# A decoder layer on one core: the last FFN projection in pairs of column blocks with seven products for eight

## The chip, the cores and the metric

The kernel runs on one core of a Trainium2 chip. The metric is the device time of one execution in microseconds; before the change it is 1440.92 us, the median of three runs (1440.82 to 1441.05).

## What is computed

One decoder layer on 256 tokens of width 2048, in float32: a combined input projection, a retention branch and a sliding-window attention branch, gates, an output projection and a layer norm, and then the channel-mixing sublayer, the only part that the change touches. Its end is

```
h = layer_norm(DEEPNORM_ALPHA * h + merged @ w_out, ln1_g, ln1_b)
ffn = (silu(h @ w_gate) * (h @ w_up)) @ w_down
h = layer_norm(DEEPNORM_ALPHA * h + ffn, ln2_g, ln2_b)
```

with `w_gate` and `w_up` 2048 x 5632 and `w_down` 5632 x 2048. Call p = silu(h @ w_gate) * (h @ w_up); it is 256 x 5632.

## The kernel before

**Products.** Every weight block and every activation is kept as a high and a low part (`wh`, `wl`, and `hh`, `hl` for h, `ph`, `pl` for the transposed p), rounded to the matmul's input type. One product of a 128 x 128 activation tile with a 128 x 512 weight block is three matmuls: high by high, high by low, low by high. All matmuls of this kind have the same size.

**Chunks.** A `Stream` walks through chunks. A plain `Chunk` is one block of 512 output columns: for every four k tiles one 1 MB weight block is loaded (`raw`), cast to `wh` by ScalarE (L217), reduced to `wl` by VectorE (L218), and used by 24 matmuls (four k tiles, two token halves, three matmuls each; L233 to L235). Its two accumulators are added to the residual by `resid` (L881).

A `PairChunk` takes two column blocks and works in k pairs: one 1 MB block holds two k tiles of both column blocks. A block of kind "s" is done as before, 8 products. A block of kind "S" is treated as a 2 x 2 matrix product (k tile by column block, token half by k tile) with seven products, in two steps: R, three products with weights as they are (9 matmuls), and T, four products with sums of weights (12 matmuls). The sums are formed by VectorE (L290, L291, L292 into `tsum`), cast by ScalarE into `th` and reduced by VectorE into `tl` (L304, L305), and the activations for them are sums too (`sh`, `sl`, made by `hsums`). Seven accumulators and an eighth for the plain blocks fill all eight PSUM banks; after the last T step `mids` (L734 to L738) combines the products P1, P5, P6 and P7, and after the last step the four C accumulators are added.

**The FFN.** There are 11 blocks of 512 columns of p, in three parts of 4, 4 and 3. For f = 0 gate and up are two plain chunks; for f = 1 to 10 they are one `PairChunk` (gate and up as the two column blocks) with eight blocks, three S and five s, in the order S s S s S s s s. After the blocks of a part come four plain chunks of `w_down` (c = 0 to 3), whose k range is that part. `done_gu` forms p for its block (L962 to L969), and `u_bg`, a background job, transposes it (L540) and splits it into `ph` and `pl` (L401, L402). The blocks of one chunk f are transposed while the next one runs; those of the last f of a part (3, 7, 10) while the first chunk of `w_down` runs.

**What sets the order.** Loads and casts are issued ahead of the matmuls as far as buffers allow: three `raw` blocks, three `wh`/`wl` pairs, one `th`/`tl` pair, one `tsum`. Background jobs advance a fixed number of steps after every step of a chunk. From this program order the framework's scheduler fixes the order of each engine's queue when the kernel is built; on the chip each queue runs in that order. A transposition, a plain matmul and an accumulator all draw on the same pool of eight banks.

Of the kernel before, what the change touches and what calls it, by code (L numbers as in the profile page):

```python
# [99 lines left out]
def layer_kernel(ctx, tc, a, out):  # L100
# [807 lines left out]
    def done_u(ch, t, c):  # L908
        sg = sgf[c]
        nc.vector.tensor_mul(out=sg[:, t], in0=sg[:, t], in1=ch.acc[t])  # L910
        if t == 0:
            pTs[c] = (sc["pp"].tile([P, 4, SEQ], F32R, name="ph"), sc["pp"].tile([P, 4, SEQ], F32R, name="pl"))
        Job(u_bg(sg, t, *pTs[c]))

    def u_bg(sg, t, ph, pl):
        yield
        yield
        ps = transpose4([sg[:, t, i * P:(i + 1) * P] for i in range(4)])
        yield
# [12 lines left out]

    def lhs_s(kp, i):
        return sc["sh"][:, i, kp], sc["sl"][:, i, kp]

    def hsums(hh, hl, sh, sl_, n):
        for kp in range(n):
            h2 = sc["tp"].tile([P, 2, 2, P], F32, name="s1")
            sm = sc["tp"].tile([P, 4, P], F32, name="vx")
            ks = slice(2 * kp, 2 * kp + 2)  # L940
            nc.vector.tensor_add(out=h2.rearrange("p k t c -> p k (t c)"), in0=hh[:, ks].bitcast(F32), in1=hl[:, ks].bitcast(F32))
            nc.vector.tensor_add(out=sm[:, 0], in0=h2[:, 0, 1], in1=h2[:, 1, 1])
            nc.vector.tensor_sub(out=sm[:, 1], in0=sm[:, 0], in1=h2[:, 0, 0])
            nc.vector.tensor_sub(out=sm[:, 2], in0=h2[:, 0, 1], in1=h2[:, 0, 0])
            nc.vector.tensor_sub(out=sm[:, 3], in0=h2[:, 1, 0], in1=sm[:, 1])
            split_evict(sh[:, :, kp], sl_[:, :, kp], sm)
            yield

    def mid_gu(ch):
# [1 line left out]
        flush()  # L951

    def flush():
        for arg in ev.pop("u", []):
            Job(u_bg(*arg))

    def done_gu(ch, f):
        acc = ch.acc
        s1, vx, w, x5 = ev["t"]
        sg = sc["fp"].tile([P, 2, C], F32, name="sg2", bufs=1)  # L960
        pTs[f] = (sc["pp"].tile([P, 4, SEQ], F32R, name="ph"), sc["pp"].tile([P, 4, SEQ], F32R, name="pl"))
        nc.vector.tensor_add(out=sg[:, 0], in0=s1, in1=acc["C11"])  # L962
        nc.scalar.activation(out=sg[:, 0], in_=sg[:, 0], func=AF.Silu)
        nc.vector.tensor_add(out=w, in0=w, in1=acc["C12"])
        nc.vector.tensor_add(out=sg[:, 1], in0=vx, in1=acc["C21"])
        nc.scalar.activation(out=sg[:, 1], in_=sg[:, 1], func=AF.Silu)
        nc.vector.tensor_mul(out=sg[:, 0], in0=sg[:, 0], in1=w)
        nc.vector.tensor_add(out=x5, in0=x5, in1=acc["C22"])
        nc.vector.tensor_mul(out=sg[:, 1], in0=sg[:, 1], in1=x5)  # L969
        ev["u"] = [(sg, t, *pTs[f]) for t in range(2)]  # L970
        if f + 1 in (4, 8, 11):
            flush()

    parts = ((0, 4), (4, 8), (8, 11))
# [24 lines left out]

    i = 0  # L1000
# [152 lines left out]
```

## Time and profile before

| | |
|---|---|
| time, median of three runs | 1440.92 us (1440.82 to 1441.05) |
| the profiled execution | 1440.99 us, of which the span of the trace is 1439.2 us |
| TensorE busy (PE) | 1432.2 us, 100% of the span |
| weight loads (PEld) | 1174.7 us, 82% |
| VectorE busy (DVE) | 1047.2 us, 73% |
| ScalarE busy (ACT) | 673.9 us, 47% |
| loaded from HBM | 271.60 MB, 190 GB/s over the span |

Busy time of PE is modelled from pipelined instructions: a matmul's row lasts 0.39 us, but the next one starts about 0.23 us after it. Whether PE loses time is therefore read from the starts of its matmuls and not from its share. On VectorE, too, rows overlap a little: an instruction takes the engine for the distance from its start to the start of the next one, if nothing is waited for.

### The profile page before, as it was taken

The page shows a single profiled execution, that of the slowest core. Times are in us where ns is not written, and L with a number is a line of the kernel's source. Part 1 is how long each engine was busy: PE and PEld are TensorE (multiplying, and loading weights), DVE is VectorE, ACT ScalarE, POOL GpSimd, SP SyncE. Part 2 cuts the span into 40 slices and gives each one's busy share as a digit, 9 for nine tenths or more (in the row PEclk, how much of TensorE's full clock was granted, in tenths as well). Part 3 has the DMA queues.
Part 4 walks back from the last instruction along what each step waited for, and adds up shares of the span by engine and source line. Part 5 has one row for each costly group of instructions (what it writes and reads, how often), then busy time and mean ns, then how long its engine had stood idle before and what let it go on. Part 6 is the DMA issues. An engine that isn't in the chain of part 4 may idle for free.

```text
span 1439.2 us, 16027 instructions
## 1 busy us (share of the span) xinstructions
PE 1432.2 (100%) x6536; PEld 1174.7 (82%) x6536; DVE 1047.2 (73%) x1127; ACT 673.9 (47%) x637; POOL 0.9 (0%) x6
## 2 busy tenths in 40 slices
PE   9999999999999999999999999999999999999998
PEld 7878888878878878788888888888888888888886
DVE  6764555487879879766688996567898755799756
ACT  5465444344545445444355454344555434454432
POOL 0000000000000000000000000000000000000000
PEclk9999999999999999999999999999999999999999
DMA  8643433455555655577445645555655555555562
GB/s 325 226 152 117 147 117 118 146 178 209 198 204 179 216 189 200 182 282 262 161 144 205 228 181 193 188 196 191 227 180 208 194 178 204 205 198 207 195 223 83
DMA packets 40233, 274.73 MB, mean 191 GB/s; under 512 B 4704, under 2 KB 4832, under 8 KB 8160
## 3 DMA queue, kind: packets, MB, share of 16 engines
q1 hardware_dynamic: 39440, 272.79, 53.3%
q8 instruction: 51, 0.84, 0.2%
q10 hardware_dynamic: 720, 0.92, 0.2%
q14 instruction: 22, 0.18, 0.0%
HBM read 271.60 MB, written 2.10 MB: 190 GB/s over the span
## 4 chain that ended last, share of the span: by engine, by line
PE 98%; DVE 1%; DMA 0%; ACT 0%; SPq 0%; issue 0%
PE bank L324 16%; PE bank L326 16%; PE bank L325 16%; PE acc L235 9%; PE acc L233 9%; PE acc L234 9%; PE bank L234 6%; PE bank L235 6%; PE bank L233 6%; PE tr L540 2%; PE mx L589 1%; PE mx L618 1%; PE bank L540 1%; DMA xraw<-in_xw 0%; PE bank L685 0%; PE mx L656 0%
## 5 line engine op out<-in xcount | busy, mean ns | idle before, releaser
L218 DVE TENSOR_TENSOR wl<-raw,wh 128x2048 fp32r<-128x2048 f32 x108 | 247.1, 2290 | 171.8 <-ACT wh L217 171.5
L304 ACT CAST wh<-raw 128x2048 fp32r<-128x2048 f32 (+1 forms) x136 | 241.2, 1773 | 229.2 <-PE bank L326 161.6
L217 ACT CAST wh<-raw 128x2048 fp32r<-128x2048 f32 x108 | 206.2, 1910 | 301.7 <-PE acc L235 108.5
L305 DVE TENSOR_TENSOR wl<-raw,wh 128x2048 fp32r<-128x2048 f32 (+1 forms) x136 | 287.0, 2115 | 61.7 <-ACT wh L304 61.2
L324 PE MATMUL bank<-wh,hh 128*128 128x512 f32 x460 | 179.6, 391 | 0.0
L326 PE MATMUL bank<-wh,hl 128*128 128x512 f32 x460 | 179.1, 389 | 0.0
L325 PE MATMUL bank<-wl,hh 128*128 128x512 f32 x460 | 179.0, 389 | 0.0
L324 PE MATMUL bank<-wh,xh 128*128 128x512 f32 x364 | 144.5, 397 | 0.0
L326 PE MATMUL bank<-wh,xl 128*128 128x512 f32 x364 | 141.8, 389 | 0.0
L325 PE MATMUL bank<-wl,xh 128*128 128x512 f32 x364 | 141.7, 389 | 0.0
L233 PE MATMUL acc<-wh,xh 128*128 128x512 f32 x352 | 141.0, 402 | 0.0
L235 PE MATMUL acc<-wh,xl 128*128 128x512 f32 x352 | 138.7, 394 | 0.0
L234 PE MATMUL acc<-wl,xh 128*128 128x512 f32 x352 | 137.9, 392 | 0.5 <-DVE wl L218 0.5
L233 PE MATMUL bank<-wh,ph 128*128 128x512 f32 x352 | 137.2, 390 | 0.0
L235 PE MATMUL bank<-wh,pl 128*128 128x512 f32 x352 | 137.0, 389 | 0.0
L234 PE MATMUL bank<-wl,ph 128*128 128x512 f32 x352 | 136.9, 389 | 0.0
L305 DVE TENSOR_TENSOR tl<-tsum,th 128x2048 fp32r<-128x2048 f32 x44 | 100.8, 2290 | 21.4 <-ACT th L304 21.1
L304 ACT CAST th<-tsum 128x2048 fp32r<-128x2048 f32 x44 | 84.2, 1914 | 63.1 <-DVE tsum L292 42.9
L326 PEld LDWEIGHTS bank<-wh,hl 128*128 128x128 f32 x460 | 86.4, 188 | 18.0
L324 PEld LDWEIGHTS bank<-wh,hh 128*128 128x128 f32 x460 | 86.4, 188 | 17.8
L325 PEld LDWEIGHTS bank<-wl,hh 128*128 128x128 f32 x460 | 86.4, 188 | 17.7
L324 PEld LDWEIGHTS bank<-wh,xh 128*128 128x128 f32 x364 | 68.3, 188 | 15.8 <-issue 1.4
(250 smaller groups left out, 2100.2 us busy)
## 6 DMA issues: line engine op xcount, KB each, us to landing
raw<-in_w_gu SPq DMA_DIRECT2D x88, 1024.0 KB, 4.9
raw<-in_w_ip SPq DMA_DIRECT2D x56, 1024.0 KB, 4.9
raw<-in_w_down SPq DMA_DIRECT2D x44, 1024.0 KB, 4.9
raw<-in_w_in SPq DMA_DIRECT2D x40, 1024.0 KB, 4.9
raw<-in_w_out SPq DMA_DIRECT2D x16, 1024.0 KB, 5.2
xraw<-in_xw SPq DMA_DIRECT2D x7, 768.0 KB, 6.7
hres<-in_x SPq DMA_DIRECT2D x1, 2048.0 KB, 7.5
out_h<-hres SPq DMA_DIRECT2D x5, 256.0 KB, 2.4
```

What stands on the lines that cost most here:

```text
L217: nc.scalar.copy(out=h[:, 0:m], in_=r)
L218: nc.vector.tensor_sub(out=l[:, 0:m], in0=r, in1=h[:, 0:m].bitcast(F32))
L233: nc.tensor.matmul(self.acc[t], lhsT=xh, rhs=wh[:, j], start=st, stop=False)
L234: nc.tensor.matmul(self.acc[t], lhsT=xh, rhs=wl[:, j], start=False, stop=False)
L235: nc.tensor.matmul(self.acc[t], lhsT=xl, rhs=wh[:, j], start=False, stop=sp)
L304: nc.scalar.copy(out=h_, in_=r)
L305: nc.vector.tensor_sub(out=l_, in0=r, in1=h_.bitcast(F32))
L324: nc.tensor.matmul(self.acc[p], lhsT=xh, rhs=wh[:, j], start=st, stop=False)
L325: nc.tensor.matmul(self.acc[p], lhsT=xh, rhs=wl[:, j], start=False, stop=False)
L326: nc.tensor.matmul(self.acc[p], lhsT=xl, rhs=wh[:, j], start=False, stop=sp)
L540: m = nc.tensor.transpose(ps[:, i], s, ident)
L589: nc.tensor.matmul(sps[u][:, i], lhsT=qT[u * HD:(u + 1) * HD, h // 2], rhs=kT[u * HD:(u + 1) * HD, g, 0:W], start=True, stop=True)
```

## The change

The four `w_down` chunks of a part become pair chunks. In parts 0 and 1, columns 0 and 1, and 2 and 3, each make one `PairChunk` of eight blocks, three of them S; in part 2, columns 0 and 1 make one of six blocks, two of them S, and columns 2 and 3 stay plain chunks. The weights are laid out for it on the host (`w_dp`, `w_dl`); the blocks stay 1 MB each and 44 in number. The sums of the transposed activations (`psh`, `psl`, two k pairs from the first block of a part, one from the second in parts 0 and 1) are made by a new background job, `psums`, queued behind the transposition of that block. The residual is now added in two steps: `mid_d` adds the four middle results to it, `done_dp` the four C accumulators (and in part 2 takes the statistics of columns 0 and 1).

```diff
-    def pair_seq(n):
+    def pair_seq(n, nkp=KT // 2):
...
-        return sq + [("s", kp) for kp in range(2 * n, KT // 2)]
+        return sq + [("s", kp) for kp in range(2 * n, nkp)]
...
+    parts = ((0, 4), (4, 8), (8, 11))
+    NS = (3, 3, 2)
...
-        Job(u_bg(sg, t, *pTs[c]))
+        ujobs.append(Job(u_bg(sg, t, *pTs[c])))
+        if t:
+            queue_p(c, ujobs)
...
-        if half == 2 and c == CP and t == 1:
-            nc.vector.tensor_mul(out=sc["zg"], in0=sc["hres"][:, t, c * C:(c + 1) * C], in1=gains["ln2_g"][:, c * C:(c + 1) * C])
...
+    def mid_d(ch, part, cp):
+        mids(ch)
+        for i, v in enumerate(ev["t"][j] for j in (0, 2, 1, 3)):
+            z = sc["hres"][:, i // 2, (2 * cp + i % 2) * C:(2 * cp + i % 2 + 1) * C]
+            if part:
+                nc.vector.tensor_add(out=z, in0=z, in1=v)
+            else:
+                nc.vector.scalar_tensor_tensor(out=z, in0=z, scalar=ALPHA, in1=v, op0=ALU.mult, op1=ALU.add)
+
+    def done_dp(ch, part, cp):
+        for t in range(2):
+            for u in range(2):
+                c = 2 * cp + u
+                z = sc["hres"][:, t, c * C:(c + 1) * C]
+                nc.vector.tensor_add(out=z, in0=z, in1=ch.acc[f"C{t + 1}{u + 1}"])
+        if part == 2:
+            for t in range(2):
+                for c in (2 * cp, 2 * cp + 1):
+                    nc.vector.bn_stats(out=sc["stats"][:, t, c], in_=sc["hres"][:, t, c * C:(c + 1) * C])
...
+    def psums(ph, pl, k0, n):
+        yield
+        yield from hsums(ph, pl, sc["psh"], sc["psl"], n, k0)
...
+    def queue_p(f, js):
+        kp = 2 * (f - f0_of[f])
+        n = min(2, ND[f] - kp)
+        if n > 0:
+            jobs["ps", f] = Job(psums(*pTs[f], kp, n), js)
...
-        for c in range(4):
-            stream.add(Chunk([a["w_down"][c, f0 + b] for b in range(nk // KB)], nk, lhs_p, lambda ch, t, part=part, c=c: done_d(ch, t, part, c),
-                             order=stagger(NSPL) if part == 2 and c == 3 else None))
+        for cp in range(2 if part < 2 else 1):
+            stream.add(PairChunk([a["w_dp"][cp, 2 * f0 + kp] for kp in range(nk // 2)], pair_seq(NS[part], nk // 2), lhs_p, lhs_ps,
+                                 lambda ch, part=part, cp=cp: mid_d(ch, part, cp), lambda ch, part=part, cp=cp: done_dp(ch, part, cp)))
+        if part == 2:
+            for c in (2, 3):
+                stream.add(Chunk([a["w_dl"][c - 2, b] for b in range(nk // KB)], nk, lhs_p, lambda ch, t, part=part, c=c: done_d(ch, t, part, c),
+                                 order=stagger(NSPL) if c == 3 else None))
```

The change moves work in the queues at three kinds of places. The first is VectorE at the end of a part. Before, at the end of chunk f = 3, p (`sg2`) is finished (L962 to L969) among the `wl` of the plain chunks:

```order
L218 TENSOR_TENSOR wl_6420<-raw_6313,wh_6419 128x2048
L962 TENSOR_TENSOR sg2_6449<-s1_6342,bank_6183 128x512
L964 TENSOR_TENSOR w_6344<-w_6344,bank_6187 128x512
L965 TENSOR_TENSOR sg2_6449<-vx_6343,bank_6203 128x512
L967 TENSOR_TENSOR sg2_6449<-sg2_6449,w_6344 128x512
L968 TENSOR_TENSOR x5_6345<-x5_6345,bank_6222 128x512
L218 TENSOR_TENSOR wl_6461<-raw_6328,wh_6460 128x2048
L969 TENSOR_TENSOR sg2_6449<-sg2_6449,x5_6345 128x512
L218 TENSOR_TENSOR wl_6507<-raw_6393,wh_6506 128x2048
L402 TENSOR_TENSOR pl_6451<-bank_6492,ph_6450 128x4x128
```

In the changed kernel the same place (L999 to L1006 there) reads, with the sums of the weights of the pair chunk in between:

```order
L305 TENSOR_TENSOR wl_6460<-raw_6345,wh_6459 128x2048
L999 TENSOR_TENSOR sg2_6489<-s1_6374,bank_6215 128x512
L1001 TENSOR_TENSOR w_6376<-w_6376,bank_6219 128x512
L1002 TENSOR_TENSOR sg2_6489<-vx_6375,bank_6235 128x512
L1004 TENSOR_TENSOR sg2_6489<-sg2_6489,w_6376 128x512
L1005 TENSOR_TENSOR x5_6377<-x5_6377,bank_6254 128x512
L292 TENSOR_TENSOR tsum_6500<-raw_6360,tsum_6500 128x512
L1006 TENSOR_TENSOR sg2_6489<-sg2_6489,x5_6377 128x512
L305 TENSOR_TENSOR wl_6505<-raw_6360,wh_6504 128x1536
L402 TENSOR_TENSOR pl_6491<-bank_6520,ph_6490 128x4x128
```

The last product (L969, now L1006) stands behind a short sum instead of a whole `wl`; on PE the eight transpositions that read it moved from behind the first 24 matmuls of the `w_down` chunk to behind its first 9 and, the second four, 5 more.

The second is VectorE in the middle of the `w_down` work. Before, in a plain chunk, the queue holds only `wl` and the two additions to the residual:

```order
L218 TENSOR_TENSOR wl_6567<-raw_6464,wh_6566 128x2048
L881 SCALAR_TENSOR_TENSOR hres_4761<-hres_4761,bank_6466 128x512
L881 SCALAR_TENSOR_TENSOR hres_4761<-hres_4761,bank_6470 128x512
L218 TENSOR_TENSOR wl_6599<-raw_6510,wh_6598 128x2048
L218 TENSOR_TENSOR wl_6631<-raw_6540,wh_6630 128x2048
```

Now, at the start of the second pair chunk of part 0 (L952 is `done_dp` of the first):

```order
L305 TENSOR_TENSOR wl_6761<-raw_6656,wh_6760 128x2048
L952 TENSOR_TENSOR hres_4761<-hres_4761,bank_6512 128x512
L952 TENSOR_TENSOR hres_4761<-hres_4761,bank_6516 128x512
L952 TENSOR_TENSOR hres_4761<-hres_4761,bank_6546 128x512
L952 TENSOR_TENSOR hres_4761<-hres_4761,bank_6565 128x512
L290 TENSOR_TENSOR tsum_6794<-raw_6671 128x1024
L305 TENSOR_TENSOR wl_6799<-raw_6671,wh_6798 128x1536
L291 TENSOR_TENSOR tsum_6794<-raw_6671,tsum_6794 128x512
L305 TENSOR_TENSOR wl_6837<-raw_6734,wh_6836 128x2048
L292 TENSOR_TENSOR tsum_6794<-raw_6671,tsum_6794 128x512
L305 TENSOR_TENSOR tl_6831<-tsum_6794,th_6830 128x2048
```

The weight sums of the chunk's second S block now stand behind the four additions, and the last of them behind the `wl` of a plain block; `tl` follows directly on it.

The third is PE in the gate and up chunk after the `w_down` work of part 0 (f = 4), at its second T step. Before:

```order
L326 MATMUL bank_6994<-wh_6982,sl_4765 128x512
L324 MATMUL bank_6998<-th_7014,sh_4764 128x512
L325 MATMUL bank_6998<-tl_7015,sh_4764 128x512
L326 MATMUL bank_6998<-th_7014,sl_4765 128x512
L324 MATMUL bank_7002<-th_7014,sh_4764 128x512
L325 MATMUL bank_7002<-tl_7015,sh_4764 128x512
```

Now:

```order
L324 MATMUL bank_7094<-th_7110,sh_4764 128x512
L324 MATMUL bank_7098<-th_7110,sh_4764 128x512
L324 MATMUL bank_7102<-th_7110,sh_4764 128x512
L324 MATMUL bank_7106<-th_7110,hh_4762 128x512
L324 MATMUL bank_7090<-wh_7116,hh_4762 128x512
L325 MATMUL bank_7090<-wl_7117,hh_4762 128x512
L326 MATMUL bank_7090<-wh_7116,hl_4763 128x512
L324 MATMUL bank_7125<-wh_7116,hh_4762 128x512
L325 MATMUL bank_7125<-wl_7117,hh_4762 128x512
L325 MATMUL bank_7094<-tl_7111,sh_4764 128x512
L326 MATMUL bank_7094<-th_7110,sl_4765 128x512
```

The four matmuls of the step that need only `th`, and five of the following plain block, moved ahead of the first that needs `tl`.

## Rows read from the trace of the kernel before

**Rows 1.** The page, parts 1 and 2: busy time, granted TensorE clock by slice.

```profile
PE 1432.2 (100%) x6536; PEld 1174.7 (82%) x6536; DVE 1047.2 (73%) x1127; ACT 673.9 (47%) x637; POOL 0.9 (0%) x6
...
PEclk9999999999999999999999999999999999999999
```

**Rows 2.** The page, part 4: shares of the chain that ended last, by engine.

```profile
PE 98%; DVE 1%; DMA 0%; ACT 0%; SPq 0%; issue 0%
```

**Rows 3.** That chain in time order (start, duration, engine, tile, line).

```profile
1052.18 0.87 PE bank L540 x8
1094.58 0.87 PE bank L540 x8
1136.96 0.87 PE bank L540 x8
1154.20 0.87 PE bank L540 x8
...
1428.93 0.24 PE bank L235
...
1434.56 0.75 DVE hres L834
```

**Rows 4.** Busy time by stretch: `w_down` of part 0, then gate/up of part 1.

```profile
core 0: us, PE busy (x) PEld busy (x) DVE busy (x) ACT busy (x) POOL busy (x), PEclk, DMA share, GB/s
892.00:980.00 88.00, 88.00 (x394) 72.97 (x393) 51.93 (x37) 33.73 (x21) 0.00 (x0) 1.00 0.56 192
...
1000.00:1128.00 128.00, 128.00 (x575) 106.14 (x574) 112.51 (x94) 66.10 (x47) 0.00 (x0) 1.00 0.56 200
```

**Rows 5.** VectorE in order of time, around the end of gate/up chunk f = 5.

```profile
1028.31 2.29 DVE L305 TENSOR_TENSOR tl<-tsum,th 128x2048 fp32r<-128x2048 f32 x1 [0.21 <-ACT th L304]
...
1056.60 1.75 DVE L305 TENSOR_TENSOR wl<-raw,wh 128x1536 fp32r<-128x1536 f32 x1
1058.27 1.22 DVE L290 TENSOR_TENSOR tsum<-raw 128x1024 f32<-128x1024 f32 x1
1059.53 0.69 DVE L291 TENSOR_TENSOR tsum<-raw,tsum 128x512 f32<-128x512 f32 x1
1060.25 0.69 DVE L292 TENSOR_TENSOR tsum<-raw,tsum 128x512 f32<-128x512 f32 x1
1060.86 2.29 DVE L305 TENSOR_TENSOR wl<-raw,wh 128x2048 fp32r<-128x2048 f32 x1
1063.06 0.68 DVE L962 TENSOR_TENSOR sg<-s,bank 128x512 f32<-128x512 f32 x1
1063.66 0.68 DVE L964 TENSOR_TENSOR w<-w,bank 128x512 f32<-128x512 f32 x1
```

**Rows 6.** PE in order of time: the second T step of chunk f = 5.

```profile
1033.65 0.39 PE L324 MATMUL bank<-th,sh 128*128 128x512 f32 x1
1033.87 0.39 PE L325 MATMUL bank<-tl,sh 128*128 128x512 f32 x1
```

**Rows 7.** VectorE making sums of activations (`hsums`) for gate/up.

```profile
749.52 0.29 DVE L942 TENSOR_TENSOR vx<-s 128x128 f32<-128x128 f32 x1
749.73 0.28 DVE L944 TENSOR_TENSOR vx<-s 128x128 f32<-128x128 f32 x1
```

**Rows 8.** ScalarE in order of time, chunk f = 4: two casts of weights.

```profile
1009.95 1.91 ACT L304 CAST th<-tsum 128x2048 fp32r<-128x2048 f32 x1 [5.21 <-DVE tsum L292]
1011.76 1.47 ACT L304 CAST wh<-raw 128x1536 fp32r<-128x1536 f32 x1
```

**Rows 9.** VectorE, then PE, in order of time at the end of part 0.

```profile
896.39 0.69 DVE L969 TENSOR_TENSOR sg<-sg,x 128x512 f32<-128x512 f32 x1
...
897.44 1.03 PE L540 MATMUL bank<-cst,sg 128*128 128x128 f32 x8
```

**Rows 10.** The page, part 6: loads of weight blocks, us from issue to landing.

```profile
raw<-in_w_gu SPq DMA_DIRECT2D x88, 1024.0 KB, 4.9
```

**Rows 11.** VectorE in the first gate/up pair chunk, f = 1: a wait for `th`.

```profile
785.33 2.29 DVE L305 TENSOR_TENSOR tl<-tsum,th 128x2048 fp32r<-128x2048 f32 x1 [2.06 <-ACT th L304]
```

More of the change, by code (lines that the diff above doesn't have):

```diff
@@ L901, in layer_kernel @@
     sgf = {}
+    ujobs = []
+    parts = ((0, 4), (4, 8), (8, 11))
+    NS = (3, 3, 2)
+    f0_of = {f: f0 for f0, f1 in parts for f in range(f0, f1)}
+    ND = {f: n for (f0, f1), n in zip(parts, NS) for f in range(f0, f1)}
     def done_g(ch, t, c):
@@ L927, in done_d, with hsums @@
         resid(ch, t, c, 1.0 if half else ALPHA, half == 2)
-        if half == 2 and c == CP and t == 1:
-            nc.vector.tensor_mul(out=sc["zg"], in0=sc["hres"][:, t, c * C:(c + 1) * C], in1=gains["ln2_g"][:, c * C:(c + 1) * C])
         if half == 2 and c == 3:
             ln2(t)
+    def mid_d(ch, part, cp):
[16 more added lines that the diff above has]
+                    nc.vector.bn_stats(out=sc["stats"][:, t, c], in_=sc["hres"][:, t, c * C:(c + 1) * C])
+            nc.vector.tensor_mul(out=sc["zg"], in0=sc["hres"][:, 1, CP * C:(CP + 1) * C], in1=gains["ln2_g"][:, CP * C:(CP + 1) * C])
     def lhs_s(kp, i):
         return sc["sh"][:, i, kp], sc["sl"][:, i, kp]
-    def hsums(hh, hl, sh, sl_, n):
+    def psums(ph, pl, k0, n):
+        yield
+        yield from hsums(ph, pl, sc["psh"], sc["psl"], n, k0)
+    def hsums(hh, hl, sh, sl_, n, k0=0):
         for kp in range(n):
@@ L945, in hsums @@
             nc.vector.tensor_sub(out=sm[:, 3], in0=h2[:, 1, 0], in1=sm[:, 1])
-            split_evict(sh[:, :, kp], sl_[:, :, kp], sm)
+            split_evict(sh[:, :, k0 + kp], sl_[:, :, k0 + kp], sm)
             yield
@@ L953, in flush @@
     def flush():
-        for arg in ev.pop("u", []):
-            Job(u_bg(*arg))
+        if "u" in ev:
+            f, args = ev.pop("u")
+            queue_p(f, [Job(u_bg(*arg)) for arg in args])
+    def queue_p(f, js):
[3 more added lines that the diff above has]
+            jobs["ps", f] = Job(psums(*pTs[f], kp, n), js)
     def done_gu(ch, f):
@@ L969, in done_gu @@
         nc.vector.tensor_mul(out=sg[:, 1], in0=sg[:, 1], in1=x5)
-        ev["u"] = [(sg, t, *pTs[f]) for t in range(2)]
+        ev["u"] = f, [(sg, t, *pTs[f]) for t in range(2)]
         if f + 1 in (4, 8, 11):
             flush()
-    parts = ((0, 4), (4, 8), (8, 11))
     seq = pair_seq(NQ)
@@ L993, in lhs_p, with lhs_ps @@
             return ph[:, k % 4, t * P:(t + 1) * P], pl[:, k % 4, t * P:(t + 1) * P]
-        for c in range(4):
-            stream.add(Chunk([a["w_down"][c, f0 + b] for b in range(nk // KB)], nk, lhs_p, lambda ch, t, part=part, c=c: done_d(ch, t, part, c),
-                             order=stagger(NSPL) if part == 2 and c == 3 else None))
+        def lhs_ps(kp, i, f0=f0):
+            assert jobs["ps", f0 + kp // 2].over
+            return sc["psh"][:, i, kp], sc["psl"][:, i, kp]
+        for cp in range(2 if part < 2 else 1):
[5 more added lines that the diff above has]
+                                 order=stagger(NSPL) if c == 3 else None))
     i = 0
@@ L1062, in layer_kernel @@
     sc["sp2"] = ppc.enter_context(tc.tile_pool(name="sp2", bufs=1, side=RIGHT))
+    pq = ppc.enter_context(tc.tile_pool(name="pq", bufs=1, side=RIGHT))
+    sc["psh"] = pq.tile([P, 4, max(NS), P], F32R, name="psh")
+    sc["psl"] = pq.tile([P, 4, max(NS), P], F32R, name="psl")
     Job(hsums(sc["hh"], sc["hl"], sc["sh"], sc["sl"], NQ))
@@ L1139 @@
         "w_gu": _pairs(g["w_gate"][0][:, C:], g["w_up"][0][:, C:]),
-        "w_down": _blocks(g["w_down"][0]),
+        "w_dp": _pairs(np.concatenate([g["w_down"][0][:, 2 * i * C:(2 * i + 1) * C] for i in range(2)], axis=1),
+                       np.concatenate([g["w_down"][0][:, (2 * i + 1) * C:(2 * i + 2) * C] for i in range(2)], axis=1)),
+        "w_dl": _blocks(g["w_down"][0][8 * C:, 2 * C:]),
         "gn_g": g["ret_gn_g"], "gn_b": g["ret_gn_b"],
```

## The prediction

> **What bounds the kernel now.** I read busy time first: PE is busy 100% of the span, VectorE 73% [rows 1]. A busy PE proves little, since its rows overlap; so next the chain that ended last, 98% of which is PE [rows 2], and then the starts of matmuls. From the transpositions at 1052.18 to those at 1094.58 lies one gate/up chunk: 183 matmuls (three S blocks of 21, five s blocks of 24) and eight transpositions in 42.40 us. From 1136.96 to 1154.20, across the end of part 1, lie 72 matmuls and eight transpositions in 17.24 us [rows 3]. The difference is 111 matmuls in 25.16 us, 0.2267 us each, and eight transpositions with what surrounds them take 0.92 us. The first T row and its neighbour start 0.22 us apart too, though the second waits for `tl` [rows 6]. PE thus has one pace in plain and pair chunks, with no gap, at a granted clock of nine tenths or more in every slice [rows 1], the 2.4 GHz level. A matmul less is 0.2267 us less, as long as nothing else becomes late.
>
> What could become late is VectorE. In the `w_down` work it is busy 51.93 of 88 us, in the gate/up chunks 112.51 of 128 [rows 4]: 59% and 88%. The change gives the first the load of the second.
>
> **The change, part by part.** *Matmuls removed.* S blocks: 2 chunks x 3 in part 0, the same in part 1, 1 x 2 in part 2, so 14, each with one product of three matmuls less: 42 x 0.2267 = 9.52 us. All of it is on the path. By the Trainium skill's page "TensorE: Matmul & The Clock Gate" (section Back-to-back issue gap) a stream of 512-column matmuls runs at about 131 ns each, or 216 ns for an isolated gap; that would make the sum 5.5 or 9.1 us. The trace's 0.2267 us decides, and is used here.
>
> *Work added on VectorE and ScalarE.* The price of an instruction is the distance to the next start [rows 5]: 2.20 for a 128x2048 `wl` or `tl`, 1.67 for 128x1536, 1.26 or less for L290, 0.72 and 0.61 for L291 and L292, 0.60 for 128x512, and 0.21 for 128x128 [rows 7]. Each S block adds sums 2.6 and `tl` 2.2 and saves 0.5 on its `wl`: 14 x 4.3 = 60 us. Each of five pairs has twelve 128x512 operations where four stood: 5 x 8 x 0.6 = 24 us. The activation sums are eight k pairs of 0.6 + 4 x 0.2 + 0.6: 16 us. Together 100 us on VectorE; ScalarE gets 14 `th` of 1.9 less 0.4 each [rows 8], and small copies, some 30 us. A `w_down` pair chunk has 183 matmuls, 41.5 us of PE, and on VectorE 3 x 2.6 + 3 x 1.67 + 8 x 2.2 + 12 x 0.6 = 37.6 us, 91%. A gate/up chunk has the same 37.6 us in 42.4 us and does not delay PE [rows 3, 4]. So the mean load fits; what counts is whether one `tl` comes late at its place.
>
> *The cover in the tight places.* Count from a chunk's first matmul: R0 lasts to 2.04, T0 to 4.76, the plain block to 10.20, R1 to 12.24, T1 to 14.96, the next plain block to 20.40, R2 to 22.44, T2 to 25.16, end 41.5. In a gate/up chunk before, `tl` for T1 ends at 1030.60 and PE reads it at 1033.87: 3.3 us of cover [rows 5, 6]. I laid the operations of the new queues end to end at these prices, each no earlier than what it reads. The tight chunks are the second pair of part 0 and the gate/up chunk behind it, and the same two in part 1. There the four `mid_d` additions push the next chunk's sums back, and the four `done_dp` additions end only at 3.3. From there: L290 to 4.4, `wl` 6.1, L291 6.7, `wl` of the plain block 8.9, L292 9.6; then VectorE waits, as it does today in chunk f = 1 [rows 11], for `th` (9.7 to 11.6), and `tl` runs 11.6 to 13.9. In plain order PE would want it at 12.47: a loss of 1.4 us. But PE has four matmuls with `th` and five of the plain block put ahead, 9 x 0.2267 = 2.04 us from 12.24, so it asks at 14.28: 0.4 us of cover. For T2: `wl` 15.6, L290 16.7, `wl` 18.9, L291 and L292 20.2, `th` to 22.1, wanted at 22.44; `tl` to 24.4, wanted, after ten matmuls put ahead, at 24.7: 0.3 us. In the gate/up chunk behind, T1 is the same; for T2 `th` stands on ScalarE behind the `wh` of a block that waits for PE's 20.4, so it ends at 24.2, wanted at 24.25 after eight matmuls put ahead, and `tl` ends at 26.9, wanted at 26.97. That is eight places with 0 to 0.4 us of cover. I charge nothing below zero: a wait that was zero cannot give time back. Upper bound: each slips by 0.5 us, 4 us in all. I take 0.05 us each, 0.4 us, near the lower end, because the prices are the same instructions' own rows.
>
> A load from HBM is part of this: the second plain block's `raw` is requested when L292 ends at 9.7 and lands 4.9 us later [rows 10], 14.6; ScalarE casts it by 16.6, VectorE wants it at 16.7. It just holds.
>
> *The ends of parts.* Before, the transpositions come 24 matmuls after the chunk's start, and `sg` (L969) ends at 897.08, 0.36 us ahead of them [rows 9]. Now PE asks for the first half after nine matmuls (2.04) and for the second at 3.6. VectorE ends these at 1.5 to 2.0 and at 3.3 to 3.7 by the same laying out. Eight transpositions become four and four, and what follows each group costs PE some 0.05 us more (0.92 against 0.87 [rows 3]). I charge 0.2 us for three ends, bounds 0 and 2.
>
> *Activation sums.* Where two k pairs fall into one chunk (f = 1, 6, 10) VectorE has 4 us more, but `tl` for T2 ends at 21.9 against 22.67, and at the following `mids` it waits for PE again. Nothing is charged. If that cover failed, a T step would wait up to 1 us, three times.
>
> *The tail* from 1428.93 to 1434.56 and beyond [rows 3] keeps its work; statistics of columns 0 and 1, and the product of L957, are done 30 us ahead of it. Zero.
>
> *Sum.* The profiled execution took 1440.99 us, a span of 1439.2 and 1.79 around it: 1439.2 - 9.52 + 0.4 + 0.2 = 1430.3, plus 1.79 = 1432.1; the median of the runs lies 0.07 lower, so **1432.0 us**.
>
> **The rivals.** *Partial.* The eight places and the three ends slip by half a microsecond and more, since every cover there is below 0.4 us. For it: the thinness. Against it: a late T gives VectorE its time back before the next, so slips do not add up. 8 x 0.5 + 3 x 0.7 = 6.1 us, hence 1437.5 us at its far end, about 1435 in its middle.
>
> *Slower: VectorE becomes the bound.* Mechanism: VectorE stands idle behind each `tl` until `th` is cast (2.06 us in [rows 11]). In the four tight chunks that is three waits of 2 us; and if operations take their whole row duration (2.29, 1.76, 0.69 [rows 5]), not the distance of starts, the work is 39.7 us. 39.7 + 6 = 45.7 against 41.5: 4.2 us lost in each of four, 16.8 us, hence 1448 us. It outweighs the gain when VectorE needs 3 us per tight chunk more than I count. For it: the wait is real, and neither `wl` nor anything else is put in between. Against it: starts, not durations, are 0.60 and 2.20 apart in runs of work [rows 5], and the third wait falls into a stretch where VectorE leads. The Trainium skill's page "PSUM — Partial Sum Buffer" (section Engine vs sequencer instructions) says that the queues of VectorE and ScalarE are strictly first in, first out. By that rule nothing can slip past a waiting `tl`; the trace agrees, as VectorE sat idle 2.06 us there.
>
> *It does not do what it says.* The blocks shrink, but pair chunks pace PE differently when their second operand is `psh`. Then up to all 9.52 us stay away: 1441 us. The rows of `sh` at PE's usual 0.22 us [rows 6] speak against it.
>
> **How the numbers follow.** 0.2% is 2.9 us, about what a measurement of this kernel can tell from no change, so "faster" ends at 1438.0. Forecast, 1431 to 1433: 0.70. Partial, 1433 to 1438: 0.20. No change, by a mixture of larger slips or the last rival: 0.05. Slower: 0.05. Faster is 0.90, same 0.05, slower 0.05. The range begins at 1430.9 (no charge at all, a little noise) and takes in the lower half of the partial case, to 1435.0: about 0.80.
>
> **What the profile after will show.** PE has 42 matmuls fewer, VectorE about 100 us more, near 1147, and ScalarE near 704. In the `w_down` stretches VectorE is busy about nine tenths. The pace stays at 0.227 us. If I am right, gaps at T1 and T2 of the second pair of parts 0 and 1, and of the chunk behind each, are under 0.1 us; if Partial, they are 0.3 to 1 us, ended by VectorE `tl`; if Slower, they are above 1.5 us and the chain of waits shows VectorE with several per cent. I am wrong if PE waits elsewhere: for a bank behind `done_dp`, or for a load.

## The result, and the profile after

| | before | after |
|---|---|---|
| time, median (range) | 1440.97 us (1440.82 to 1441.05) | 1432.53 us (1432.37 to 1432.67) |
| span of the trace | 1439.2 us | 1430.7 us |
| TensorE busy | 1432.2 us, 6536 instructions | 1423.1 us, 6494 |
| VectorE busy | 1047.2 us | 1135.0 us |
| ScalarE busy | 673.9 us | 699.3 us |

The ratio is 0.9942 (95% interval 0.993 to 0.9953): the change made the kernel 8.4 us faster, to 1432.5 us where 1432.0 was predicted.

The page of the changed kernel, parts 1, 2 and 4 (busy time, granted clock by slice, the chain's shares by engine), to be held against [rows 1, 2]:

```profile
PE 1423.1 (99%) x6494; PEld 1165.0 (81%) x6494; DVE 1135.0 (79%) x1271; ACT 699.3 (49%) x664; POOL 0.9 (0%) x6
...
PEclk9999999999999999999999999999999999999999
...
PE 98%; DVE 1%; DMA 0%; ACT 0%; SPq 0%; issue 0%
```

The chain is TensorE's as before, with 42 instructions fewer, although VectorE took on 88 us. The chain of the changed kernel in order of time (start, duration, what):

```profile
1420.46 0.24 PE bank L235
...
1426.09 0.75 DVE hres L834
```

In [rows 3] the last matmul is at 1428.93 and the last addition at 1434.56; both came 8.47 us earlier, so the tail of 5.63 us is untouched. Busy time of the changed kernel by stretch, the stretches of [rows 4]:

```profile
core 0: us, PE busy (x) PEld busy (x) DVE busy (x) ACT busy (x) POOL busy (x), PEclk, DMA share, GB/s
892.00:980.00 88.00, 88.00 (x393) 72.57 (x392) 77.37 (x70) 44.97 (x30) 0.00 (x0) 1.00 0.56 203
1000.00:1128.00 128.00, 128.00 (x573) 105.77 (x572) 120.41 (x115) 69.29 (x52) 0.00 (x0) 1.00 0.57 204
```

VectorE's share in the `w_down` work went from 59% (51.93 of 88 us) to 88% (77.37), and in the gate/up stretch from 88% (112.51 of 128 us) to 94% (120.41); TensorE stays busy throughout.

**Where 42 matmuls went.** At 0.2267 us they are 9.52 us; 8.47 arrived, so 1.05 us was given back. I summed, over all pairs of neighbouring 128x512 matmuls from the first gate/up pair chunk to the last matmul of `w_down`, what their starts lie apart beyond 0.2267 us. By chunk, 0.98 us of it lies in four chunks in which run e7_nomid below has none: the second pair chunk of parts 0 and 1 (0.13 and 0.12 us) and the gate/up chunk behind each (f = 4 and 8, 0.37 and 0.36 us). These are the chunks that the prediction calls tight. In part 0 they look like this. First VectorE and ScalarE in the second pair chunk, at its steps T1 and T2 (start, duration, engine, line, operation; in brackets the idle time before and what ended it):

```profile
943.34 0.68 DVE L292 TENSOR_TENSOR tsum<-raw,tsum 128x512 f32<-128x512 f32 x1
944.13 1.91 ACT L304 CAST th<-tsum 128x2048 fp32r<-128x2048 f32 x1 [5.53 <-DVE tsum L292]
946.08 2.29 DVE L305 TENSOR_TENSOR tl<-tsum,th 128x2048 fp32r<-128x2048 f32 x1 [2.05 <-ACT th L304]
...
954.01 0.69 DVE L292 TENSOR_TENSOR tsum<-raw,tsum 128x512 f32<-128x512 f32 x1
956.75 2.29 DVE L305 TENSOR_TENSOR tl<-tsum,th 128x2048 fp32r<-128x2048 f32 x1 [2.05 <-ACT th L304]
```

Then PE where it first reads each of these two `tl`:

```profile
948.68 0.39 PE L325 MATMUL bank<-tl,psh 128*128 128x512 f32 x1
...
959.17 0.42 PE L325 MATMUL bank<-tl,psh 128*128 128x512 f32 x1
```

`tl` ends at 948.37 and 959.04, so the cover (from the end of `tl` to its first use) is 0.31 and 0.13 us. T1 loses nothing, T2 about 0.1 us. In the gate/up chunk behind it T2 is worse. Its `th` on ScalarE, and PE around it:

```profile
996.72 1.91 ACT L304 CAST wh<-raw 128x2048 fp32r<-128x2048 f32 x1 [4.63 <-PE bank L326]
998.54 1.91 ACT L304 CAST th<-tsum 128x2048 fp32r<-128x2048 f32 x1
...
1000.11 0.39 PE L325 MATMUL bank<-wl,hh 128*128 128x512 f32 x1
1000.50 0.96 PE L324 MATMUL bank<-th,sh 128*128 128x512 f32 x3
```

ScalarE stood for 4.63 us before a `wh` that waits for PE, and `th` stands behind it; it ends at 1000.45, and PE's matmul starts 0.39 us after its neighbour in place of 0.23. That place costs 0.3 us (the next start is late by 0.11 us too), its twin in f = 8 as much.

### The profile page after: what moved, and what is told of

Read it like the earlier page. It is cut to its first block, busy times and chain, and to the rows that moved or that the text cites. A ratio compares the mean times of both kernels' runs of the same rounds, so it can differ in the third digit from the quotient of the medians.

```text
span 1430.7 us, 16141 instructions
## 1 busy us (share of the span) xinstructions
PE 1423.1 (99%) x6494; PEld 1165.0 (81%) x6494; DVE 1135.0 (79%) x1271; ACT 699.3 (49%) x664; POOL 0.9 (0%) x6
## 4 chain that ended last, share of the span: by engine, by line
PE 98%; DVE 1%; DMA 0%; ACT 0%; SPq 0%; issue 0%
PE bank L324 21%; PE bank L326 21%; PE bank L325 21%; PE acc L235 9%; PE acc L233 9%; PE acc L234 9%; PE tr L540 2%; PE mx L589 2%; PE mx L618 1%; PE bank L540 1%; PE bank L235 1%; PE bank L234 1%; PE bank L233 1%; DMA xraw<-in_xw 0%; PE bank L685 0%; PE mx L656 0%
## 5 line engine op out<-in xcount | busy, mean ns | idle before, releaser
L304 ACT CAST wh<-raw 128x2048 fp32r<-128x2048 f32 (+1 forms) x174 | 307.7, 1769 | 295.1 <-PE bank L326 223.8
L305 DVE TENSOR_TENSOR wl<-raw,wh 128x2048 fp32r<-128x2048 f32 (+1 forms) x174 | 366.4, 2108 | 62.0 <-ACT wh L304 61.6
L218 DVE TENSOR_TENSOR wl<-raw,wh 128x2048 fp32r<-128x2048 f32 x70 | 160.1, 2288 | 79.6 <-ACT wh L217 79.3
L217 ACT CAST wh<-raw 128x2048 fp32r<-128x2048 f32 x70 | 133.5, 1909 | 175.0 <-PE acc L235 110.8
L305 DVE TENSOR_TENSOR tl<-tsum,th 128x2048 fp32r<-128x2048 f32 x58 | 132.6, 2287 | 34.2 <-ACT th L304 34.0
L304 ACT CAST th<-tsum 128x2048 fp32r<-128x2048 f32 x58 | 111.0, 1914 | 95.1 <-DVE tsum L292 78.0
L324 PE MATMUL bank<-wh,ph 128*128 128x512 f32 x220 | 85.9, 390 | 0.0
L325 PE MATMUL bank<-wl,ph 128*128 128x512 f32 x220 | 85.6, 389 | 0.0
L326 PE MATMUL bank<-wh,pl 128*128 128x512 f32 x220 | 85.1, 389 | 0.0
```

Source lines behind the costliest of these rows:

```text
L217: nc.scalar.copy(out=h[:, 0:m], in_=r)
L218: nc.vector.tensor_sub(out=l[:, 0:m], in0=r, in1=h[:, 0:m].bitcast(F32))
L304: nc.scalar.copy(out=h_, in_=r)
L305: nc.vector.tensor_sub(out=l_, in0=r, in1=h_.bitcast(F32))
L324: nc.tensor.matmul(self.acc[p], lhsT=xh, rhs=wh[:, j], start=st, stop=False)
L325: nc.tensor.matmul(self.acc[p], lhsT=xh, rhs=wl[:, j], start=False, stop=False)
```

## The experiments

All are edits of the changed kernel. The times below are medians of four or more runs that lie within 0.7 us of each other, unless a range is given with the run; the ratios to the kernel before are known to about 0.12%, which is 1.7 us, so where two kernels differ by less than that the conclusion rests on whether their runs overlap and on the place in the trace.

| run | what | time, us |
|---|---|---|
| e4_form | pairs of columns, no S block | 1440.94 |
| e1_seven | S blocks 2, 2, 2 | 1434.22 |
| changed kernel | S blocks 3, 3, 2 | 1432.53 |
| e2_third | 3, 3, 3 | 1432.38 |
| e3_four | 4, 4, 3 | 1440.09 |
| e5_dose2, e6_dose7 | 2 or 7 idle additions more at a chunk's end | 1432.50, 1432.65 |
| e7_nomid | middle additions left out | 1431.37 |
| e8_nosums | activation sums left out | 1432.52 |
| e9_pool, e10_pool333, e11_pool443 | middle additions on GpSimd; S as named | 1434.54, 1434.14, 1438.08 |
| e12_nomid443 | middle additions left out, S 4, 4, 3 | 1430.90 |

**Is it the seven products? (e4_form, e1_seven.)** Two rivals are tested here: that the pair form itself moves the time, and that VectorE already sets the pace.

```diff
-    NS = (3, 3, 2)
+    NS = (0, 0, 0)
```

(with the scaling by ALPHA moved into the closing additions, since there is no middle step)

> The columns go in pairs, with the pairs' layout, banks and additions at the ends, but with no S block at all: 24 matmuls in every block, so as many matmuls as the kernel before, no weight sums, no sums of activations, no additions in the middle. My theory (the form costs only 0.2 us at the ends of parts): 1441.0 to 1441.4. Rival (pair chunks pace PE differently, or four banks closed at once hold PE up): 1442 or more, or a gain below 1440.5 that has nothing to do with the seven products.

Measured 1440.94 us against 1440.98 for the kernel before: the form is free. The ends of parts are not tested by this as the changed kernel has them: in e4_form the eight transpositions stay together behind 24 matmuls.

```diff
-    NS = (3, 3, 2)
+    NS = (2, 2, 2)
```

> S blocks 2, 2, 2 in the three parts in place of 3, 3, 2: ten S blocks in all, not fourteen, so 12 matmuls more than the changed kernel. My theory (PE sets the end at 0.2267 us per matmul, VectorE is late only by tenths at a few T steps): 12 x 0.2267 = 2.72 us more, and at most 0.6 us of the give-back returns, because VectorE has 4.3 us less work in each pair chunk: 1434.6 to 1435.3. Rival (VectorE already sets the pace in the tight chunks): the third S block of each pair bought little, so the time rises by less than 1.5 us, below 1434.

Measured 1434.22 us, 0.4 below my range and 0.2 above the rival's 1434. Against the kernel before that is 6.76 us for 30 matmuls, 0.225 us each: the first ten S blocks earn their full price, and nothing is given back. (An estimate from the 131 ns of the Trainium skill's page "TensorE: Matmul & The Clock Gate", section Back-to-back issue gap, is 3.9 us, one from its 216 ns 6.5 us; the measured 6.76 us is nearest to the second, and above both.) The last four, the third S block of each pair in parts 0 and 1, earn 1.69 of 2.72 us. So all of the give-back comes with the third S block.

**What takes the 1 us back? (e7_nomid, e8_nosums.)**

```diff
-            if part:
-                nc.vector.tensor_add(out=z, in0=z, in1=v)
-            else:
-                nc.vector.scalar_tensor_tensor(out=z, in0=z, scalar=ALPHA, in1=v, op0=ALU.mult, op1=ALU.add)
+            pass
```

> The four additions in the middle of each pair chunk are left out (so the output lacks what they add to the residual): 2.4 us less of VectorE in each of five chunks. My theory (PE waits for tl only by tenths): the waits at T1 and T2 of the tight chunks go, 0.3 to 0.8 us less: 1431.7 to 1432.2. Rival (VectorE is the bound there): some 2 us less in each of four chunks, 1424 to 1426.

Measured 1431.37 us: 1.16 us less, 0.3 beyond my range and far from the rival's 6 us and more. Against the kernel before as it was measured with this run (1440.85 us) the gain is 9.48 us, all but 0.04 of what 42 matmuls are worth. The waits at T1 and T2 are gone. The same T2 as above, VectorE and then PE in this run:

```profile
951.44 2.29 DVE L305 TENSOR_TENSOR tl<-tsum,th 128x2048 fp32r<-128x2048 f32 x1 [0.47 <-ACT th L304]
...
956.73 0.39 PE L324 MATMUL bank<-th,psh 128*128 128x512 f32 x1
956.95 0.39 PE L325 MATMUL bank<-tl,psh 128*128 128x512 f32 x1
```

The cover is 3.22 us here, the 3.3 us that the gate/up chunks had before [rows 5, 6]; with the 2.4 us of `mid_d` it is 0.13. These four additions are what makes the chunks tight, as the prediction's laying out had it.

```diff
-        if n > 0:
+        if n > 9:
             jobs["ps", f] = Job(psums(*pTs[f], kp, n), js)
...
-            return sc["psh"][:, i, kp], sc["psl"][:, i, kp]
+            return sc["sh"][:, i, kp], sc["sl"][:, i, kp]
```

> The sums of the transposed activations are left out, and the T steps of w_down read the sums of the gate/up input in their place (so the output is another): 16 us less on VectorE, same matmuls. My theory (they lie beside PE's work and cost nothing): 1432.3 to 1432.5. Rival (they make the T steps of the chunks in which they run late): up to 1 us in each of three parts, 1429.5 to 1431.5.

Measured 1432.52 us: the activation sums, some 15 us of VectorE (it is busy 1120.1 us without them, 1135.0 with them), cost nothing.

**How much room does VectorE have? (e5_dose2, e6_dose7.)** Here I expected a cover of 0.1 us to mean that any further work is paid one for one.

```diff
+        if part < 2:
+            for _ in range(7):
+                zz = sc["tp"].tile([P, C], F32, name="zz")
+                nc.vector.tensor_add(out=zz, in0=z, in1=z)
```

(at the end of `done_dp`; two additions in e5_dose2)

> Two more 128x512 additions on VectorE behind the four that end each pair chunk of parts 0 and 1 (their result goes nowhere): 1.2 us of VectorE ahead of T1 in four chunks, the second pair of each part and the gate/up chunk behind it. My theory (the covers at T1 stand near zero, from 0 to 0.1 us): nearly all of it is paid four times, 4 x 1.1 = 4.4 us: 1436.9 (1435.5 to 1437.5). Rival (VectorE has 41.5 - 37.6 = 4 us of slack per chunk and takes it in): 1432.5 to 1433.

> Seven more additions at the same four places, 4.2 us each. My theory (paid one for one once the cover is gone): 4 x 4.1 = 16.4 us: 1449 (1446 to 1450), slower than the kernel before. Rival (4 us of slack per chunk, so the first 4 us are free): 1433 to 1434.

Measured 1432.50 and 1432.65 us, against 1436.9 and 1449 expected. My theory of the cover fell. VectorE of e6_dose7 in the second pair chunk of part 0, the place of the rows above:

```profile
938.65 0.68 DVE L956 TENSOR_TENSOR zz<-hres 128x512 f32<-128x512 f32 x1
939.25 0.69 DVE L291 TENSOR_TENSOR tsum<-raw,tsum 128x512 f32<-128x512 f32 x1
939.85 0.68 DVE L956 TENSOR_TENSOR zz<-hres 128x512 f32<-128x512 f32 x1
940.45 0.68 DVE L292 TENSOR_TENSOR tsum<-raw,tsum 128x512 f32<-128x512 f32 x1
941.05 0.69 DVE L956 TENSOR_TENSOR zz<-hres 128x512 f32<-128x512 f32 x1
...
943.33 0.69 DVE L956 TENSOR_TENSOR zz<-hres 128x512 f32<-128x512 f32 x1
943.93 2.29 DVE L305 TENSOR_TENSOR tl<-tsum,th 128x2048 fp32r<-128x2048 f32 x1
```

Four of the seven additions stand ahead of `tl` for T1, and yet it starts at 943.93, not at 946.08. The scheduler put L292 ahead of two `wl`, so that `th` was cast while VectorE worked, and the wait of 2.05 us for it disappeared. Busy time of e6_dose7 in this chunk and the next:

```profile
937.00:978.00 41.00, 41.00 (x183) 33.96 (x182) 40.57 (x39) 19.58 (x13) 0.00 (x0) 1.00 0.60 219
978.00:1020.00 42.00, 41.99 (x186) 34.45 (x185) 41.31 (x40) 21.53 (x15) 0.00 (x0) 1.00 0.57 204
```

VectorE is at 98% and more, and TensorE does not wait in the first of them and under 0.3 us in the second. In part 1 the second pair chunk loses nothing either, but the gate/up chunk behind it (f = 8) waits at T2. ScalarE, then PE there:

```profile
1249.88 1.92 ACT L304 CAST wh<-raw 128x2048 fp32r<-128x2048 f32 x1 [5.08 <-DMA raw<-in_w_gu]
1251.70 1.91 ACT L304 CAST th<-tsum 128x2048 fp32r<-128x2048 f32 x1
...
1253.66 0.98 PE L324 MATMUL bank<-th,sh 128*128 128x512 f32 x3 [0.74 <-ACT th L304]
```

`th` stands behind a `wh` whose load came late, and with the start after it PE loses 1.0 us. In all, the four tight chunks lose 1.36 us in e6_dose7 where the changed kernel loses 0.98: 16.8 us of added work cost 0.4 us. In e5_dose2 it is 0.82 us, 0.69 of it at one place, T2 of f = 4, where PE waits for `tl`. So a thin cover in a scheduled order says when the instruction was placed, not how much more the engine can take. A limit of this test: the order was made anew for each dose, so what a dose would cost in the order of the changed kernel was not measured, and why only one of the two gate/up chunks waits long in each dose is open.

**More S blocks (e2_third, e3_four).**

```diff
-    NS = (3, 3, 2)
+    NS = (3, 3, 3)
```

> S blocks 3, 3, 3: one S block more, in part 2 alone, where VectorE waits longer between pieces of work. My theory: three matmuls less, 0.68 us, all of it on the path: 1431.8 (1431.6 to 1432.1). Rival (any further S block finds VectorE too late): 1432.5 or above.

Measured 1432.38 us: 0.15 of the 0.68 us. The rival is nearer. VectorE and PE of this run at the last T step of part 2:

```profile
1377.57 2.29 DVE L305 TENSOR_TENSOR tl<-tsum,th 128x2048 fp32r<-128x2048 f32 x1 [2.05 <-ACT th L304]
1379.91 0.50 PE L325 MATMUL bank<-tl,psh 128*128 128x512 f32 x1 [0.28 <-DVE tl L305]
```

Again 2.05 us of waiting for `th` ahead of `tl`, and PE starts 0.67 us after the matmul before it, 0.44 us late (and 0.11 at the next start).

```diff
-    NS = (3, 3, 2)
+    NS = (4, 4, 3)
```

> S blocks 4, 4, 3: five S blocks more, 15 matmuls less, 3.4 us of PE. A pair chunk of parts 0 and 1 then has 180 matmuls, 40.8 us, and on VectorE 37.6 + 4.3 = 41.9 us. My theory: in the second pair of parts 0 and 1, whose covers stand near zero, the added 4.3 us are paid in full, 8.6 us, and the gate/up chunks behind gain and lose nothing: 1432.5 - 3.4 + 8.6 = 1437.7 (1434 to 1441), with gaps above 1 us at T steps ended by tl. Rival (PE alone bounds the kernel, VectorE's share is only a share): 1429.1.

Measured 1440.09 us (1437.48 to 1440.69): five S blocks more turn the gain of 8.4 us into next to none. The eleven runs fall into groups: three, whose mean granted TensorE clock is 1.000, took 1437.5 to 1437.6 us, and the eight with 0.997 or 0.998 took 1439.3 to 1440.7. The three are what I expected (1437.7); the 2.4 us by which the median lies higher go with the lower clock, to which the last section comes back. The direction and the gaps are as expected. The chain of e3_four by engine, in a run with 0.997:

```profile
PE 90%; DVE 6%; issue 2%; ACT 2%; DMA 0%; SPq 0%; ACTq 0%; DVEq 0%
```

VectorE in it at the border to the gate/up chunk f = 4:

```profile
975.62 0.69 DVE L945 SCALAR_TENSOR_TENSOR hres<-hres,s 128x512 f32<-128x512 f32 x1
...
976.82 0.69 DVE L945 SCALAR_TENSOR_TENSOR hres<-hres,w 128x512 f32<-128x512 f32 x1
...
978.03 0.69 DVE L945 SCALAR_TENSOR_TENSOR hres<-hres,x 128x512 f32<-128x512 f32 x1
978.63 2.28 DVE L305 TENSOR_TENSOR tl<-tsum,th 128x2048 fp32r<-128x2048 f32 x1
980.83 2.29 DVE L305 TENSOR_TENSOR wl<-raw,wh 128x2048 fp32r<-128x2048 f32 x1
```

and PE behind it:

```profile
980.97 0.50 PE L325 MATMUL bank<-tl,sh 128*128 128x512 f32 x1 [1.22 <-DVE tl L305]
981.30 0.40 PE L326 MATMUL bank<-th,sl 128*128 128x512 f32 x1
983.17 0.80 PE L325 MATMUL bank<-wl,hh 128*128 128x512 f32 x1 [1.47 <-DVE wl L305]
983.76 0.63 PE L326 MATMUL bank<-wh,hl 128*128 128x512 f32 x1
```

The four `mid_d` additions stand ahead of `tl` and of a plain block's `wl`, and PE waits for both. This is the Slower rival's mechanism.

**Taking the middle additions off VectorE (e9 to e12).** In the pool runs `mid_d` uses GpSimd, which is idle there.

```diff
-                nc.vector.tensor_add(out=z, in0=z, in1=v)
+                nc.gpsimd.tensor_add(out=z, in0=z, in1=v)
             else:
-                nc.vector.scalar_tensor_tensor(out=z, in0=z, scalar=ALPHA, in1=v, op0=ALU.mult, op1=ALU.add)
+                nc.gpsimd.tensor_scalar(out=z, in0=z, scalar1=ALPHA, scalar2=None, op0=ALU.mult)
+                nc.gpsimd.tensor_add(out=z, in0=z, in1=v)
```

> The four additions in the middle of each w_down pair chunk go to GpSimd, which has nothing else to do there (in part 0 a scaling and an addition in place of one combined operation); the output is the same sum. My theory now (the give-back of about 1 us is VectorE's 2.4 us of these additions, which shrink the time between the end of tl and its first use at T1 and T2 from 3.2 us to 0.1 us): as without them, 1431.4 (1431.2 to 1431.9). Rival (GpSimd is late for the additions at the chunk's end, or its work makes VectorE's instructions longer): 1432.5 to 1436.

> The same, with S blocks 3, 3, 3. My theory: the third S block of part 2 cost VectorE its cover (0.05 us at its last T step, a wait of 0.44 us); with 2.4 us of VectorE taken away it earns its three matmuls, 0.68 us: 1430.7 (1430.5 to 1431.3). Rival (the last T step is late because its loads or casts are late, not VectorE): 1431.3 to 1432.4.

> The same, with S blocks 4, 4, 3. VectorE then has 41.9 - 2.4 = 39.5 us of work in the 40.8 us of a pair chunk. My theory (the loss with four S blocks, 11 us, was VectorE's overload at the border of two chunks): most of it goes, 1430 to 1434. Rival (the loss comes from the place of the fourth T step right ahead of the chunk's end, with the combining additions due at once): 1436 to 1440.

Measured 1434.54 (1434.06 to 1435.38), 1434.14 (1433.06 to 1435.82) and 1438.08 us (1437.87 to 1439.61). The first two are slower than with the additions on VectorE; the rival that GpSimd lengthens VectorE's instructions is right. GpSimd and VectorE in e9_pool (spans on GpSimd are rough), near the end of the second pair chunk of part 0:

```profile
967.54 1.29 POOL L946 TENSOR_TENSOR hres<-hres,vx 128x512 f32<-128x512 f32 x1
968.47 2.51 DVE L305 TENSOR_TENSOR tl<-tsum,th 128x2048 fp32r<-128x2048 f32 x1 [0.74 <-ACT th L304]
968.79 3.34 POOL L946 TENSOR_TENSOR hres<-hres,x 128x512 f32<-128x512 f32 x1
970.90 2.85 DVE L305 TENSOR_TENSOR wl<-raw,wh 128x1536 fp32r<-128x1536 f32 x1
```

A 128x1536 `wl` lasts 1.75 us in e7_nomid, 2.85 us here; from 700 us on, every one that runs beside GpSimd's work in e9_pool takes 2.84 or 2.85 us and every other one 1.74 to 1.76. An addition on GpSimd lasts 1.29 us in one row and 3.34 in the next. The third row ends 1.15 us after `tl` does (972.13 against 970.98), and `wl` ends 1.62 us after that: it reads as if each worked while the other stood. The Trainium skill's page "SBUF — State Buffer" (section Terms) says that VectorE and GpSimd arbitrate for a shared port pair whose lock is held for a whole instruction, and that the loser "fully blocks"; these rows agree. VectorE thus got back nothing of the 2.4 us per chunk (busy 1136.1 us in e9_pool, 1135.0 with the additions on VectorE), and PE waits 0.3 to 0.6 us at three other places.

In e10_pool333 PE still starts 0.57 us late at the last T step of part 2, as in e2_third; with this disturbance that does not yet clear the middle additions. Two runs with three S blocks in part 2 do: PE starts 0.33 us late there in e3_four, with these additions on VectorE, and 0.32 us late in e12_nomid443, without them. My theory for that step fell too, and its cause stays open. e11_pool443 is 2.0 us below the median of e3_four, but no faster than the three runs of e3_four at the full clock (1437.5 us), so it shows no gain and does not tell load from place. The last run left the additions out:

> S blocks 4, 4, 3 and the four additions in the middle of each w_down pair chunk left out (so the output lacks what they add to the residual), not moved to another engine. VectorE has 39.5 us of work in the 40.8 us of a pair chunk, and no other engine works beside it on the same tiles. Theory 'load' (four S blocks lost because VectorE had 41.9 us of work for 40.8): the loss is gone, 15 matmuls less than the run without these additions and three S blocks: 1431.37 - 3.4 = 1428.0, up to 1430. Theory 'place' (the fourth T step ends 5.4 us ahead of the chunk's end, so that the combining additions, the closing additions and the next chunk's first sums all fall together): waits of 1 us and more remain at the chunk borders, 1432 or more.

Measured 1430.90 us, between the two theories: 9.2 us less than e3_four (6.6 less than its three runs at the full clock), 2.9 us short of what 57 matmuls fewer should give (1440.95 - 12.92 = 1428.0). The `tl` of the rows above, and its first use, in this run:

```profile
979.17 2.29 DVE L305 TENSOR_TENSOR tl<-tsum,th 128x2048 fp32r<-128x2048 f32 x1
...
982.05 0.39 PE L325 MATMUL bank<-tl,sh 128*128 128x512 f32 x1
```

The cover is 0.59 us and PE does not wait for `tl` there; what stays are six places in the tight chunks where PE waits for `th`, 0.3 us each, and 0.4 us at the last T step of part 2. So 12 us of VectorE (five times 2.4) cost 6.6 us of time with four S blocks, 9.2 with the lower clock, and 1.2 us with three. Nor is VectorE's mean load the measure. In e3_four, by stretches of the second pair chunk of part 0 and the one behind it, it is busy less than in e6_dose7, which lost 0.3 us in the same two chunks:

```profile
937.00:979.00 42.00, 40.53 (x178) 32.90 (x177) 39.25 (x36) 20.26 (x13) 0.00 (x0) 1.00 0.54 199
979.00:1021.00 42.00, 39.31 (x166) 31.73 (x165) 39.50 (x31) 18.54 (x11) 0.00 (x0) 0.96 0.56 202
```

This is 93 and 94% with PE idle for 4.2 us, there 98% and more with PE idle for 0.01 us. What counts, as far as these runs go, is whether work stands ahead of a `tl` (or, in f = 8 of e6_dose7, a `th`) that has no cover left. That the same additions behind those `tl` would be free with four S blocks wasn't tried.

None of these kernels that does the whole computation beats the changed kernel by more than e2_third's 0.15 us, which its runs (1432.34 to 1432.67) do not tell from nothing.

## Why the prediction was right, point by point

**The pace and the price of a matmul: right.** 42 x 0.2267 = 9.52 us was the whole of the gain, and e1_seven and e4_form show that it comes from the seven products alone: 30 matmuls bring 6.76 us, none bring none.

**The cover in the tight places: the mechanism right, the term too small.** It was charged 0.4 us and measured 0.98. The laying out gave 0.4 us of cover at T1 and 0.3 at T2 of the second pair chunk; measured 0.31 and 0.13. In the gate/up chunk behind it gave `th` for T2 the end 24.2 us after the chunk's start; with that start at 975.8 (892.0, then two chunks of 183 matmuls and eight transpositions) it came at 24.6, and PE waited 0.3 us for it, not for `tl`. What failed is the step "0.05 us each, near the lower end": two of the eight places took 0.3 us each, the others 0 to 0.15. The sign given for this (gaps under 0.1 us if right, 0.3 to 1 us ended by VectorE's `tl` if Partial) holds, or nearly, at six places; at these two the starts are late by 0.28 us, and it was ScalarE's `th` that ended the wait. Estimates that end within 0.4 us of a deadline cannot be charged at nearly nothing. That `mid_d` pushes the sums back is shown by e7_nomid (cover 3.22 us without it).

**The ends of parts: sized too large.** Charged 0.2 us. PE at the end of part 0:

```profile
894.02 0.60 PE L540 MATMUL bank<-cst,sg 128*128 128x128 f32 x4
894.37 0.48 PE L324 MATMUL bank<-wh,ph 128*128 128x512 f32 x1
894.69 0.40 PE L325 MATMUL bank<-wl,ph 128*128 128x512 f32 x1
```

From the last matmul before a group to the second one behind it, less two matmuls, a group of four takes 0.447 us and a group of eight 0.885: two groups of four cost 0.01 us more than one of eight, 0.03 us for three ends. PE starts both groups 0.23 us after the matmul before, so it does not wait for `sg`.

**Activation sums and tail: right at zero.** e8_nosums, and the 5.63 us of tail.

**VectorE's work: 14% too much.** The prediction added 100 us; 87.8 were added, by 144 instructions as counted. By what each instruction takes up to the next start, the S blocks brought 51 us for the 60 counted, the additions 21 for 24 and the activation sums 16 for 16. The 1.26 and 0.72 us taken for L290 and L291 in [rows 5] held small gaps; and where more instructions follow each other directly, every row overlaps the next by 0.09 us, so the `wl` of 128x2048 came down too (from 2.24 to 2.22 us each, from 700 us on). ScalarE was given 30 us more and got 25.4.

**The rivals.** *Partial* had the right places and 0 to 0.3 us where it allowed 0.5. *It does not do what it says* is out by e4_form and e1_seven. *Slower* named a mechanism that exists: e3_four has it, with `tl` 1.4 us late. But its threshold, 3 us more per tight chunk, is wrong as it was put: 4.2 us more in e6_dose7 cost 0.4 us over all four. It counted the waits for `th` (2.05 us at T1 and T2) as lost time of VectorE. They are room: the order of e6_dose7 filled them. That nothing slips past a waiting `tl` was seen again (2.05 us of idle VectorE at T1 and T2 of the changed kernel); but which work stands in the queue was settled when the kernel was built.

The sum of the two charges was 0.6 us and came to 1.05: 0.98 in the tight places, 0.03 at the ends, under 0.1 elsewhere. Hence 1432.5, not 1432.0 us. In part the two errors cancel: one term was 0.6 us too small, the other 0.2 us too large.

## What to carry to other kernels

If one engine paces a kernel without gaps, the price of an instruction removed from it is the spacing of its starts, and what has to be worked out is at which few places another engine's result is due, not that engine's share. A thin cover in an order that a scheduler made says where it put the work, and not how much more fits: add work and look again; what hurts is work that stands in the queue ahead of a result that is due. Use such a saving until the give-back per step nears the saving: here the first ten steps earned their full 0.68 us each, the next four 0.42, the fifteenth at most 0.15, and with nineteen nearly the whole gain was gone (at the full clock 3.5 us of it were left).

## What the hardware showed that I had not expected

In e3_four two waits of PE were followed by a lower clock. Busy time of e3_four in three stretches, the columns as in the windows above (the clock stands third from the end):

```profile
979.36:983.17 3.81, 1.12 (x4) 0.30 (x2) 3.81 (x3) 1.90 (x1) 0.00 (x0) 0.94 0.01 4
983.17:986.20 3.03, 3.03 (x7) 2.44 (x8) 3.03 (x5) 0.00 (x0) 0.00 (x0) 0.52 0.68 203
986.20:989.00 2.80, 2.80 (x13) 2.26 (x12) 2.80 (x4) 0.00 (x0) 0.00 (x0) 1.00 0.37 155
```

PE was busy 1.12 of 3.81 us; then the granted clock is 0.52, near the 1.2 GHz level, with matmuls 0.43 us apart, and after seven of them it is back at 1.00. The two waits, 3.0 us together, cost some 1.5 us more in that way. The same happened at the border to f = 8. Twice 1.5 us is what lies between the three runs of e3_four with a mean clock of 1.000 (1437.5 us) and most of the others (1440.4; the one with 0.998 lies between, at 1439.3): the same kernel came out 3 us apart, and by an estimate from these rows the lowered clock accounts for it; no trace of one of the three was kept, so that is not shown. A single wait of 1.6 us ahead of 938.9, in the same trace, did not lower the clock: it is 1.00 from 936.0 to 942.0.

GpSimd's additions, in tiles that VectorE does not touch at that moment, lengthened VectorE's 128x1536 `wl` from 1.75 to 2.85 us, and in the rows shown its own 128x512 addition took 1.29 and 3.34 us.
